# A two-block transformer stack on one core: six changes to the order of work around starts, merges, norms and the last column

## The chip, the cores and the metric

The kernel runs on one core of one Trainium2 chip. The metric is device time in microseconds (us) from launch to end. The engines are named as in the profile: PE is TensorE (PEld its weight loads), DVE is VectorE, ACT is ScalarE, POOL is GpSimd, SP is SyncE, which issues most DMAs.

## What is computed

512 tokens of width 1024 go through two blocks of two layers each, all in float32.

```python
def first_block(x, ...):          # block 1, for l in range(2)
        h = rmsnorm(x, norm1_g[l])
        p = h @ w_in[l]
        ...
        branches = jnp.stack([y_rw, y_ret, y_sg], axis=2)
        proj = jnp.einsum('bsgc,gcd->bsgd', branches, w_branch[l])
        gates = jax.nn.sigmoid(gate_logits.reshape(B, S, N_BRANCH, D_MODEL))
        x = x + jnp.sum(gates * proj, axis=2) @ w_out[l]
        x = x + conv_ffn(rmsnorm(x, norm2_g[l]), ...)
    return rmsnorm(x, final_g)
```

The three branches of block 1 are an RWKV-7 recurrence (y_rw), a chunked retention (y_ret) and a spatial gating unit (y_sg). Block 2 has five attention branches in place of these (dsa, fox, sb, nsa, mem), the same gated merge over five branches with an output projection, and no feed-forward part; it ends with a last RMSNorm, which is the result.

## The kernel before

**Products.** x lies with features on the partitions: eight tiles of 128 x 512 (features x tokens). A float32 product is made as three products of split operands: every operand is cut into an upper part (whi of a weight, shi or shl of an activation), rounded on ACT, and a lower one (wlo, slo), a subtraction on DVE. mm3 (L166) does whi x shi, whi x slo and wlo x shi into one PSUM bank, so lines L168, L169 and L170 are most of PE's work. fm_tile (L361) makes one output tile of 128 features from 8 blocks of weights, 24 matmuls over 512 tokens; fm_steps (L370) is the same as a generator. Weights come in chunks of 128 x 1024 (8 blocks) through weights (L152): a DMA on SP's queue into wraw, the cast to whi on ACT (L159), the subtraction for wlo on DVE (L160). Each of wraw, whi and wlo has two buffers.

**PSUM.** Three pools share the eight banks. In block 1 dense tiles (pm and pbr, from PM) have two banks, small products (psx, psn, psb and others, from P) four, and retention (PF) two; in block 2 PM has three and P five.

**The order of work.** In block 1 the three branches and the gates are generators that a small planner (Plan) interleaves: each step names a cost and a wait, chains that are due come first, and dense tiles fill in. PE's order there is the order in which the program issues. Everywhere else the framework orders each engine's instructions by program order and by its own model of when each would be ready; every queue then runs in that order. The casts of weights and the evacuations of dense tiles have raised priority.

**Places that the change touches.**

- The start (run, L1782): for each of the eight x tiles norm_step makes the two parts (L184, L185) and at once the square (L299, ACT) and its sum (L302, DVE); two weight chunks are loaded ahead. Then come constants, some of them through F buffers, of which there are eight and which the x tiles use too, and end_norm: the sums over features as products with ones (psn, L310), a root (ACT), a reciprocal (DVE), and a broadcast by products with the identity (psb, L317) into rb. Dense tiles are scaled with rb when they leave PSUM, so a tile's matmuls need only the parts, and its bank is free only when rb is there.
- tm_group (L379): values with tokens on the partitions, 256 features wide. Both weight chunks are loaded, and then each of four token groups gets 24 matmuls over 256 columns (12 from each chunk), a bank, and an evacuation on ACT (L788, L839). There are four such groups in each layer of block 1.
- rw_unit (L609): one of 32 units of the recurrence, each for 128 tokens of one pair of heads. Its last products are psx: for each 64-token half c (rows of the array) and head e (columns of the array) three products of 64 x 64 x 64, each of them two passes in the trace. Halves go to different banks, heads to different partitions of a bank.
- merge (L923): for each of 8 output columns c and each branch n a gate is loaded (L933), made a tanh on ACT (L936) and multiplied on DVE (L939) with pbr, a product of 12 matmuls; the branch sums are added (L943). In block 1 the third branch is the recurrence, whose last part (shl, L181) is the last thing that the planner's chains make (L739 to L757 in rw_final, with sums that are broadcast through DRAM).
- Between the blocks: ffn (L963) ends with end_norms (L325), two norms at once: psn for both sums, five small operations, psb twice, rb and rb1. Block 2 then starts with the projections misc and iq (col, L1297).
- The end: the last merge keeps its eight output columns (xlast), end_norm follows, and at L1816 each column is scaled on DVE and sent out in one DMA, on SP's and ACT's queue in turn.

## Time and profile before

| what | us |
|---|---|
| median of 3 runs | 3305.34 (3305.04 to 3309.78) |
| the profiled execution, its own time | 3305.33 |
| its span, first to last instruction | 3303.6 |
| PE busy | 3231.0 |
| DVE busy | 2188.8 |
| ACT busy | 1365.9 |
| POOL busy | 125.6 |

The span is that of one execution under the profiler; the time of the same execution is 1.7 us longer than its span. Busy times are unions of instructions on an engine. Matmuls are pipelined, so a busy PE is not PE at its peak: how far apart matmuls start tells more than how long one lasts.

### The profile page before, as it was taken

Reading aid. Unit: us, or ns where it says so; the run is one execution under the profiler, and the core shown is the slowest. Engines: PE = TensorE matmul, PEld = TensorE weight load, DVE = VectorE, ACT = ScalarE, POOL = GpSimd, SP = SyncE. Lnnn points to the kernel's source line nnn. Section 1 sums busy time; section 2 is a strip of 40 time slices with the busy share of each in tenths; the row PEclk is TensorE's granted clock in tenths of the full one; section 3 lists DMA queues with packets and bytes.
Section 4 is the critical chain, followed back from the end, with each engine's and each line's share of the span. In section 5 each row is a group of like instructions: output and inputs, shape, how many; then the busy total and the mean of one; then the engine's idle time right before and its main releaser. Section 6 shows DMA issues by size and latency. Waiting matters only on the chain.

```text
span 3303.6 us, 47422 instructions
## 1 busy us (share of the span) xinstructions
PE 3231.0 (98%) x17956; PEld 2594.5 (79%) x17960; DVE 2188.8 (66%) x4062; ACT 1365.9 (41%) x2440; POOL 125.6 (4%) x176
## 2 busy tenths in 40 slices
PE   8999999999999999999999999999999999999998
PEld 6787877888887787878888878877787888777777
DVE  6765656777537855646677446986666669866665
ACT  5433434444335333434444334344334443443443
POOL 0000000000000000000000000010003100100031
PEclk9999999999999999999999999999999999999999
DMA  4433245333433423246333437453455564533464
GB/s 146 124 94 96 74 136 170 128 107 96 137 112 105 130 75 91 80 139 189 102 99 99 150 108 212 134 159 104 121 185 197 172 170 138 152 113 121 152 209 140
DMA packets 198644, 434.75 MB, mean 132 GB/s; under 512 B 29704, under 2 KB 56456, under 8 KB 198416
## 3 DMA queue, kind: packets, MB, share of 16 engines
q1 hardware_dynamic: 197328, 429.62, 42.1%
q8 instruction: 142, 2.33, 0.3%
q0 software_dynamic: 512, 1.05, 0.1%
q10 hardware_dynamic: 576, 1.05, 0.1%
q14 instruction: 86, 0.70, 0.1%
HBM read 339.05 MB, written 61.36 MB: 121 GB/s over the span
## 4 chain that ended last, share of the span: by engine, by line
PE 84%; DVE 6%; DMA 6%; ACT 2%; issue 2%; SPq 1%; POOL 0%; DVEq 0%; ACTq 0%; POOLq 0%
PE pm L168 22%; PE pm L170 21%; PE pm L169 21%; PE psy L1152 2%; PE pbr L168 2%; PE pbr L169 2%; PE pbr L170 2%; PE pspt L1142 2%; DVE wlo L160 1%; PE psl L1124 1%; DMA sqr<-sumd 1%; PE psl L1125 1%; DMA rdw<-sumd 1%; ACT whi L159 1%; PE pssc L804 1%
## 5 line engine op out<-in xcount | busy, mean ns | idle before, releaser
L168 PE MATMUL pm<-shi,whi 128*128 128x512 f32 x3072 | 1231.7, 401 | 8.8 <-ACT whi L159 7.9
L170 PE MATMUL pm<-shi,wlo 128*128 128x512 f32 x3072 | 1207.4, 393 | 1.1 <-DVE wlo L160 1.0
L169 PE MATMUL pm<-slo,whi 128*128 128x512 f32 x3072 | 1206.1, 393 | 1.8 <-DVE slo L185 1.8
L159 ACT ACTIVATE whi<-wraw 128x1024 fp32r<-128x1024 f32 x480 | 509.3, 1061 | 884.4 <-PE pm L169 533.3
L160 DVE TENSOR_TENSOR wlo<-wraw,whi 128x1024 fp32r<-128x1024 f32 x480 | 588.1, 1225 | 206.1 <-ACT whi L159 199.6
L168 PEld LDWEIGHTS pm<-shi,whi 128*128 128x128 f32 x3072 | 578.6, 188 | 147.4 <-issue 26.8
L170 PEld LDWEIGHTS pm<-shi,wlo 128*128 128x128 f32 x3072 | 578.1, 188 | 127.6 <-DVE wlo L160 4.8
L169 PEld LDWEIGHTS pm<-slo,whi 128*128 128x128 f32 x3072 | 578.7, 188 | 117.2 <-DVE slo L185 4.4
L424 DVE TENSOR_TENSOR ev<-pm,rb 128x512 f32<-128x512 f32 x140 | 96.1, 686 | 113.6 <-PE pm L170 113.1
L894 DVE TENSOR_TENSOR gate<-pm,rb 128x512 f32<-128x512 f32 x80 | 55.1, 688 | 128.5 <-PE pm L170 128.4
L168 PE MATMUL pbr<-shi,whi 128*128 128x512 f32 x288 | 115.0, 399 | 14.0 <-ACT shl L181 10.4
L168 PE MATMUL pm<-whi,shi 128*128 128x256 f32 x384 | 115.0, 300 | 7.1 <-ACT whi L159 7.1
L169 PE MATMUL pm<-wlo,shi 128*128 128x256 f32 x384 | 111.7, 291 | 3.7 <-DVE wlo L160 3.6
L170 PE MATMUL pbr<-shi,wlo 128*128 128x512 f32 x288 | 113.1, 393 | 0.0
L169 PE MATMUL pbr<-slo,whi 128*128 128x512 f32 x288 | 113.1, 393 | 0.0
L170 PE MATMUL pm<-whi,slo 128*128 128x256 f32 x384 | 111.1, 289 | 0.0
L939 DVE SCALAR_TENSOR_TENSOR gate<-gate,pbr 128x512 f32<-128x512 f32 x128 | 85.8, 683 | 31.8 <-PE pbr L170 31.1
L943 POOL TENSOR_TENSOR gate<-gate 128x512 f32<-128x512 f32 x48 | 78.3, 1630 | 593.1 <-DVE gate L939 337.0
L936 ACT ACTIVATE gate<-gate 128x512 f32<-128x512 f32 x128 | 75.9, 626 | 42.2 <-DMA gate<-gtd 39.9
L1109 ACT ACTIVATE p<-psl,st 128x256 f32<-128x256 f32 (+3 forms) x128 | 65.2, 513 | 61.0 <-DVE st L1107 51.6
L168 PEld LDWEIGHTS pm<-whi,shi 128*128 128x128 f32 x384 | 76.0, 198 | 9.8 <-ACT whi L159 7.7
L169 PEld LDWEIGHTS pm<-wlo,shi 128*128 128x128 f32 x384 | 76.3, 199 | 4.7 <-DVE wlo L160 4.5
(506 smaller groups left out, 4465.8 us busy)
## 6 DMA issues: line engine op xcount, KB each, us to landing
wraw<-in_w_gt SPq DMA_DIRECT2D x148, 512.0 KB, 3.7
wraw<-in_w_in SPq DMA_DIRECT2D x116, 512.0 KB, 3.7
wraw<-in_f_up SPq DMA_DIRECT2D x88, 512.0 KB, 3.5
gtd<-gate SPq DMA_DIRECT2D x116, 256.0 KB, 2.0
gate<-gtd SPq DMA_DIRECT2D x116, 256.0 KB, 4.0
wraw<-in_w_br SPq DMA_DIRECT2D x44, 512.0 KB, 3.7
wraw<-in_f_dn SPq DMA_DIRECT2D x44, 512.0 KB, 3.5
wraw<-in_w_out SPq DMA_DIRECT2D x32, 512.0 KB, 3.7
```

The source lines that it names most:

```text
L159: nc.scalar.activation(hi[:, :n], raw[:, :n], AF.Copy)
L160: nc.vector.tensor_tensor(lo[:, :n], raw[:, :n], hi[:, :n].bitcast(F32), op=OP.subtract)
L168: nc.tensor.matmul(ps, lhsT=lhs[0], rhs=rhs[0], start=first, stop=False, skip_group_check=skip)
L169: nc.tensor.matmul(ps, lhsT=lhs[0], rhs=rhs[1], start=False, stop=False, skip_group_check=skip)
L170: nc.tensor.matmul(ps, lhsT=lhs[1], rhs=rhs[0], start=False, stop=last, skip_group_check=skip)
L424: self.last = self.nc.vector.tensor_tensor(t, ps, self.rb, op=OP.mult)
L936: nc.scalar.activation(g, g, AF.Tanh, scale=0.5)
L939: nc.vector.scalar_tensor_tensor(g, g, 1.0, pb, op0=OP.add, op1=OP.mult)
L943: (nc.gpsimd if self.pre and n in self.cfg.get("pa", (1, 2, 3)) else nc.vector).tensor_tensor(g, g, acc, op=OP.add)
L1109: nc.scalar.activation(p[:, :w], l, AF.Exp, bias=st[:, 0:1], accum_out=st[:, 1:2])
L1142: nc.tensor.transpose(pt_[:, b * 128:(b + 1) * 128], ps[e][:, b * 128:(b + 1) * 128], self.ident)
L1152: nc.tensor.matmul(psy[64 * e:64 * e + 64, :], lhsT=vs[e][b], rhs=pts[e][:, b * 128:(b + 1) * 128], start=first and b == 0, stop=last and ...
```

## The change

Six edits. (1) At the start the parts of all x tiles come first and the squares after them; the first two dense tiles take retention's two banks. (2) tm_group holds two banks and uses the first weight chunk for all four token groups before it takes the second. (3) psx takes two banks at once and goes through the products with head and half as the inner loops, so that products that follow each other lie in different quadrants of the array. (4) In merges of three branches the third branch's product of a column comes after the first two products of the next column; the weights are laid out in the same order. (5) end_norms moves from the end of ffn into block 2, behind the first two projection tiles. (6) The last output column and the last norm are made by halves of the tokens (finish), each half with its own sums, root, scaling and DMAs.

```diff
     def fm_steps(self, ws):
 
-        ps = self.PM(name="pm")
+        ps = self.banks.pop(0) if self.banks else self.PM(name="pm")
...
     def tm_group(self, src, evac):
...
-        ws = [self.weights(src[i], 1024) for i in range(2)]
-        for g in range(4):
-            ps = self.PM([128, 512])
-            for k in range(KD):
-                w = ws[k // 4]
-                o = (k % 4) * 256
-                hh = (self.h[k][0][:, g * 128:(g + 1) * 128], self.h[k][1][:, g * 128:(g + 1) * 128])
-                self.mm3(ps[:, :256], hh, (w[0][:, o:o + 256], w[1][:, o:o + 256]), k == 0, k == KD - 1)
-                if k == KD // 2 - 1:
+        ps = [self.PM([128, 2, 256]) for _ in range(2)]
+        for i in range(2):
+            w = self.weights(src[i], 1024)
+            for g in range(4):
+                for k in range(4):
+                    hh = [t[:, g * 128:(g + 1) * 128] for t in self.h[4 * i + k]]
+                    ww = [t[:, k * 256:(k + 1) * 256] for t in w]
+                    self.mm3(ps[g // 2][:, g % 2], hh, ww, i == 0 and k == 0 and g % 2 == 0, i == 1 and k == 3, skip=True)
+                if i and g % 2:
+                    evac(g - 1, ps[g // 2][:, 0])
+                    evac(g, ps[g // 2][:, 1])
+                if (i, g) != (1, 3):
                     yield MORE
-            evac(g, ps[:, :256])
-            yield MORE if g < 3 else TILE
+        yield TILE
...
+        psx = [self.P([128, 2, 64], "psx") for _ in range(2)]
+        for m in range(3):
+            for e in range(2):
+                for c in range(2):
+                    cs = slice(64 * c, 64 * c + 64)
+                    os = ws = slice(64 - 64 * e, 128 - 64 * e)
+                    us = slice(64 * e, 64 * e + 64)
+                    b_ = tk[cs, 0, us]
+                    o, x, y, first, last = ((0, uw[cs, e, ws], b_, True, True), (1, b_, uw[cs, e, us], True, False),
+                                            (1, tk[cs, 1, us], vp[cs, 3 * e, :], False, True))[m]
+                    nc.tensor.matmul(psx[c][os, o, :], lhsT=x, rhs=y, start=first, stop=last, skip_group_check=True)
         for c in range(2):
-            psx = self.P([128, 2, 64], "psx")
...
-                nc.tensor.matmul(psx[os, 0, :], lhsT=uw[cs, e, ws], rhs=b_, start=True, stop=True,
-                                 skip_group_check=True)
-                nc.tensor.matmul(psx[os, 1, :], lhsT=b_, rhs=uw[cs, e, us], start=True, stop=False,
-                                 skip_group_check=True)
-                nc.tensor.matmul(psx[os, 1, :], lhsT=tk[cs, 1, us], rhs=vp[cs, 3 * e, :], start=False, stop=True,
-                                 skip_group_check=True)
...
+            nc.vector.tensor_tensor(xt[:, 2 * g + c, :], psx[c][:, 0], self.ident64, op=OP.add)
+            nc.scalar.activation(cc[:, 2 * g + c, :], psx[c][:, 1], AF.Copy)
...
-        s, late = [], []
...
-        for c in range(KD):
-            acc = None
-            for n in range(nb):
-                if (c, n) in self.gd:
-                    g = self.F(name="gate")
-                    nc.sync.dma_start(g, self.gd[c, n])
-                else:
-                    g = self.gate(self.gs, "F")
-                nc.scalar.activation(g, g, AF.Tanh, scale=0.5)
-                pb = self.fm_tile(ws, ys[n], name="pbr")
-                with self.tc.high_priority(offset=self.cfg.get("hp", self.AHEAD)):
-                    nc.vector.scalar_tensor_tensor(g, g, 1.0, pb, op0=OP.add, op1=OP.mult)
-                if late and n == self.cfg.get("ln", 1):
-                    s.append(self.split(late.pop(), *stag(c - 1), scale=0.5))
-                if acc is not None:
...
-            self.dump("%ss%d_%d" % (self.pre, l, c), acc)
-            late.append(acc)
-        s.append(self.split(late.pop(), *stag(c), scale=0.5))
+        for c, n in merge_order(nb):
+            if (c, n) in self.gd:
+                g = self.F(name="gate")
+                nc.sync.dma_start(g, self.gd[c, n])
+            else:
+                g = self.gate(self.gs, "F")
+            nc.scalar.activation(g, g, AF.Tanh, scale=0.5)
+            pb = self.fm_tile(ws, ys[n], name="pbr")
+            with self.tc.high_priority(offset=self.cfg.get("hp", self.AHEAD)):
+                nc.vector.scalar_tensor_tensor(g, g, 1.0, pb, op0=OP.add, op1=OP.mult)
+            if late and n == self.cfg.get("ln", 1):
+                s.append(self.split(late.pop(), *stag(len(s)), scale=0.5))
+            if c in acc:
+                (nc.gpsimd if self.pre and n in self.cfg.get("pa", (1, 2, 3)) else nc.vector).tensor_tensor(
+                    g, g, acc[c], op=OP.add)
+            acc[c] = g
+            if n == nb - 1:
+                self.dump("%ss%d_%d" % (self.pre, l, c), g)
+                late.append(acc.pop(c))
+        for t in late:
+            s.append(self.split(t, *stag(len(s)), scale=0.5))
...
-        for c in range(KD):
+        for c in range(KD if split else KD - 1):
...
+        if not split:
+            self.finish(wo, s)
+
+    def finish(self, wo, s):
+
+        nc = self.nc
+        ww = [next(wo) for _ in range(KD)]
+        self.xlast.append(self.x_get(KD - 1))
+        x = self.xlast[-1]
+        for hf in range(2):
+            cs = slice(256 * hf, 256 * hf + 256)
+            ps = self.PM()
+            for k in range(KD):
+                self.mm3(ps[:, 0:256], ww[k], [t[:, cs] for t in s[k]], k == 0, k == KD - 1)
+            nc.vector.tensor_tensor(x[:, cs], ps[:, 0:256], x[:, cs], op=OP.add)
+            sq = self.T_(name="sql")
+            nc.scalar.activation(sq[:, 0:256], x[:, cs], AF.Square)
+            ps = self.P([128, 512], "psn")
+            for g in range(2):
+                for i, t in enumerate((self.sq[:, cs], sq)):
+                    nc.tensor.matmul(ps[:, g:g + 1], lhsT=t[:, g * 128:(g + 1) * 128], rhs=self.ones[:, 0:1],
+                                     start=i == 0, stop=i == 1, skip_group_check=True)
+            col = self.hp.tile([128, 8], F32, name="rcol", tag="rcol", bufs=2)
+            nc.scalar.activation(col[:, 4:6], ps[:, 0:2], AF.Sqrt, bias=self.eps[:, 0:1], scale=1.0 / D)
+            nc.vector.reciprocal(col[:, 0:2], col[:, 4:6])
+            ps = self.P([128, 512], "psb")
+            for g in range(2):
+                nc.tensor.matmul(ps[:, g * 128:(g + 1) * 128], lhsT=col[:, g:g + 1].to_broadcast([128, 128]),
+                                 rhs=self.ident, start=True, stop=True)
+            for c, t in enumerate(self.xlast):
+                nc.vector.scalar_tensor_tensor(t[:, cs], t[:, cs], self.vlast(c), ps[:, 0:256], op0=OP.mult, op1=OP.mult)
+                (nc.sync if c % 2 else nc.scalar).dma_start(self.out[c][:, cs], t[:, cs])
...
-        if gain1:
-            self.end_norms()
-        else:
+        if not gain1:
             self.end_norm()
...
+        self.early = []
+        if l == 0 and self.sq2 is not None:
+            self.early = [self.fm_tile(self.ws) for _ in range(2)]
+            self.end_norms()
...
-        self.end_norm(copy=gain is not None)
+        if gain is not None:
+            self.end_norm()
...
     def col(self, name, scale=None, tag="F"):
-        return self.evac2(self.fm_tile(self.ws), name, scale, tag)
+        ps = self.early.pop(0) if self.early else self.fm_tile(self.ws)
+        return self.evac2(ps, name, scale, tag)
...
                 with block(self, "act"):
                     self.begin_norm()
                     self.first = self.stream(I["w_in1"][0, 0:14])
+                    xs = []
                     for c in range(KD):
-                        self.norm_step(c, self.x_get(c), vg(0)(c), eng=nc.gpsimd if c in self.cfg.get("pe", ()) else None)
+                        xs.append(self.x_get(c))
+                        self.h.append(self.split(xs[c], tag="h", scale=vg(0)(c)))
                         if c in self.cfg.get("pr", (0, 2)):
                             self.first.prime()
+                    for x in xs:
+                        self.sq = self.add_square(self.sq, x)
+                    self.banks = [self.PF(), self.PF()]
                     self.consts()
                     self.end_norm()
                     self.am = [self.ap.tile([128, 2, 4, 128], F32, name="am%d" % i) for i in range(2)]
...
+                self.vlast = vg(40)
                 for l in range(L2):
                     self.block2_layer(l, vg(32) if l < L2 - 1 else None)
-                for c, x in enumerate(self.xlast):
-                    nc.vector.scalar_tensor_tensor(x, x, vg(40)(c), self.rb, op0=OP.mult, op1=OP.mult)
-                    (nc.sync if c % 2 else nc.scalar).dma_start(self.out[c], x)
...
-def merge_stream(w):
+def merge_order(nb):
+
+    if nb != 3:
+        return [(c, n) for c in range(8) for n in range(nb)]
+    o = []
+    for c in range(9):
+        o += [(c, 0), (c, 1)] * (c < 8) + [(c - 1, 2)] * (c > 0)
...
```

## Rows read from the trace of the kernel before

**Rows 1.** The page, sections 1 and 4: busy time; the last chain
```profile
...
PE 3231.0 (98%) x17956; PEld 2594.5 (79%) x17960; DVE 2188.8 (66%) x4062; ACT 1365.9 (41%) x2440; POOL 125.6 (4%) x176
...
PE 84%; DVE 6%; DMA 6%; ACT 2%; issue 2%; SPq 1%; POOL 0%; DVEq 0%; ACTq 0%; POOLq 0%
...
```

**Rows 2.** What PE waited for: in total, times, longest us
```profile
...
PE pm L168 <- ACT whi L159: 15.0, 4, 7.9
PE pbr L168 <- ACT shl L181: 10.4, 2, 5.4
...
PE pm L169 <- DVE wlo L160: 3.6, 2, 2.1
...
PE psx L697 <- ACT cc L704: 0.2, 1, 0.2
...
```

**Rows 3.** Busy time by stretch; third from the end: granted clock
```profile
...
123.77:129.33 5.56, 5.56 (x26) 5.56 (x27) 1.37 (x4) 1.04 (x3) 0.00 (x0) 0.50 0.54 151
1087.76:1091.89 4.13, 4.13 (x19) 4.13 (x20) 1.15 (x2) 1.40 (x4) 0.00 (x0) 0.50 0.17 46
514.66:518.45 3.79, 3.79 (x9) 3.05 (x10) 0.65 (x1) 0.38 (x1) 0.00 (x0) 0.50 0.00 0
1480.38:1484.42 4.04, 4.04 (x10) 3.18 (x11) 0.90 (x2) 0.63 (x1) 0.00 (x0) 0.50 0.00 0
1942.24:1956.53 14.29, 7.30 (x33) 7.01 (x33) 10.51 (x27) 9.26 (x18) 4.15 (x17) 0.64 0.44 139
...
```

**Rows 4.** Timeline, token-major groups: start, duration, operation, [idle before]
```profile
...
116.47 0.28 PE L168 MATMUL pm<-whi,shi 128*128 128x256 f32 x1
...
121.32 0.38 PE L168 MATMUL pm<-whi,shi 128*128 128x256 f32 x1 [3.26 <-ACT whi L159]
...
122.50 1.22 DVE L160 TENSOR_TENSOR wlo<-wraw,whi 128x1024 fp32r<-128x1024 f32 x1
...
2043.35 0.50 PE L168 MATMUL pm<-whi,shi 128*128 128x256 f32 x2 [1.19 <-ACT whi L159]
...
```

**Rows 5.** Busy time and counts of pbr, first merge to PE's stop
```profile
...
498.80:509.62 10.82, 10.80 (x45) 8.42 (x45) 1.38 (x2) 1.00 0.38 114
...
```

**Rows 6.** Timeline of DVE in the first merge
```profile
...
511.19 0.69 DVE L752 TENSOR_TENSOR y<-y,rdw 128x512 f32<-128x512 f32 x1 [3.76 <-DMA rdw<-sumd]
...
```

**Rows 7.** Timeline of PE, one unit's psx products and what follows
```profile
...
239.10 0.33 PE L697 MATMUL psx<-tk,uw 64*64 64x64 f32 x2
...
239.27 0.27 PE L697 MATMUL psx<-tk,uw 64*64 64x64 f32 x1
239.33 0.22 PE L699 MATMUL psx<-uw,tk 64*64 64x64 f32 x1
...
240.10 0.38 PE L168 MATMUL pm<-whi,shi 128*128 128x256 f32 x1
...
```

**Rows 8.** Busy time and counts of psam in one unit
```profile
...
246.08:246.50 0.42, 0.42 (x16) 0.42 (x16) 0.00 (x0) 1.00 1.02 419
...
```

**Rows 9.** Timeline of PE between the blocks
```profile
...
1945.91 3.54 PE L331 MATMUL psn<-ones,sq 128*128 128x1 f32 x16 [3.67 <-DVE sq L302]
1951.87 3.75 PE L192 MATMUL psb<-c_ident,rcol 128*128 128x128 f32 x16 [2.42 <-DVE rcol L340]
1956.53 0.47 PE L168 MATMUL pm<-shi,whi 128*128 128x512 f32 x1 [0.90 <-DVE rb L346]
...
```

**Rows 10.** Timeline, all engines, first tile of the kernel
```profile
...
13.59 0.91 SPq L155 DMA_DIRECT2D wraw<-in_w_in  x2
...
17.40 0.50 PE L169 MATMUL pm<-slo,whi 128*128 128x512 f32 x1 [0.30 <-DVE slo L185]
...
18.66 0.50 PE L169 MATMUL pm<-slo,whi 128*128 128x512 f32 x1 [0.30 <-DVE slo L185]
...
```

**Rows 11.** Timeline of DVE after the last matmul of the last column
```profile
...
3287.85 0.69 DVE L954 TENSOR_TENSOR x<-pm,x 128x512 f32<-128x512 f32 x1 [3.30 <-PE pm L170]
...
3294.66 5.36 DVE L1816 SCALAR_TENSOR_TENSOR x<-x,vecg,psb 128x512 f32<-128x512 f32 x8 [2.23 <-PE psb L317]
```

More of the change, by code (lines that the diff above doesn't have):

```diff
@@ L117, in __init__ @@
         self.dbg_outs = dbg or {}
+        self.banks = []
+        self.sq2 = None
         self.cfg = cfg or {}
@@ L925, in merge @@
         nb = len(ys)
[L926 removed]
+        s, late, acc = [], [], {}
         ws = self.stream(wbr[l])
[L928 to L947 removed]
+        for c, n in merge_order(nb):
[19 more added lines that the diff above has]
+            s.append(self.split(t, *stag(len(s)), scale=0.5))
         self.begin_norm()
@@ L1920, with merge_stream @@
 ORDER1 = [1, 2, 0]
-def merge_stream(w):
+def merge_order(nb):
[4 more added lines that the diff above has]
+        o += [(c, 0), (c, 1)] * (c < 8) + [(c - 1, 2)] * (c > 0)
+    return o
+def merge_stream(w, order=None):
     t = []
-    for c in range(8):
-        for n in range(w.shape[0]):
-            t += list(w[n][:, c * 128:(c + 1) * 128].reshape(-1, 128, 128))
+    for c, n in order or [(c, n) for c in range(8) for n in range(w.shape[0])]:
+        t += list(w[n][:, c * 128:(c + 1) * 128].reshape(-1, 128, 128))
     return np.stack(t).reshape(-1, 8, 128, 128).transpose(0, 2, 1, 3).reshape(-1, 128, 1024)
@@ L2038, in layout @@
                            for l in range(L)])
-    o["w_br1"] = np.stack([merge_stream(I["w_branch"][l][ORDER1]) for l in range(L)])
+    o["w_br1"] = np.stack([merge_stream(I["w_branch"][l][ORDER1], merge_order(3)) for l in range(L)])
     o["w_out1"] = np.stack([np.stack(_fm(I["w_out"][l], range(0, 1024, 128))) for l in range(L)])
```

9 lines of the change are left out of this document (removed).

## The prediction

> **What bounds the kernel now.** I read the page first. TensorE (PE) is busy for 98% of the span and holds 84% of the chain that ended last; no other engine holds more than 6% of it [rows 1]. So the time is PE's work plus the short stretches in which PE stands still, and an edit is worth what it takes out of those two. PE is busy for 3231.0 of 3303.6 us, so some 72 us of standing still are to be had at most, beside work that is done faster.
>
> The second view, PE's list of waits [rows 2], names the places. 15.0 us are spent waiting for the upper weight part whi, in four waits; the longest, 7.9, is the start of the kernel. 10.4 us in two waits go to shl, the parts of a recurrent branch, at the two merges of block 1. 3.6 us go to wlo.
>
> The third view, busy time and granted clock by stretch [rows 3], shows that a wait costs more than its length. [...] Work at half speed costs half of the stretch again.
>
> **What the sum is made against:** the profiled execution's 3305.33 us, its span of 3303.6 plus 1.7 outside. The median of the runs is 3305.34, the same number.
>
> **Token-major groups in chunks (tm_group).** The old order finishes one token group with both weight chunks before the next, so the second chunk is wanted after 12 matmuls: the group starts at 116.47, and PE stands at 121.32 for 3.26 us on whi and then for wlo, whose subtraction starts at 122.50 and takes 1.22 [rows 4]. The new order uses the first chunk for four token groups, 48 matmuls at a pitch of 0.12, before it wants the second. In the two layers the old order costs: whi 15.0 less the start (7.9) less one wait in block 2 (1.2, the last row of [rows 4]), so 5.9; wlo 3.6; half of the 5.56 and 4.13 us at half clock, 4.8. Together 14.3. The new need for wlo is at 116.47 + 48 x 0.12 + 0.12 = 122.35, and wlo is there at 123.72, so about 1.4 us stay in the first layer; I take 0.4 for the second. Gain 12.5, between 8 (the clock still falls) and 14.3. The number of matmuls is unchanged. Both pm banks are now held for the whole group; the first is handed back 24 matmuls, 2.9 us, before the end, which is the cover that each bank has today.
>
> **The lagging third branch (merge order).** PE does 45 pbr matmuls between 498.80 and 509.62 and then stops [rows 5]. In program order the stop would come after 12 + 12 + 9, so one tile of the next column is already done ahead of its turn. The new order places four tiles and nine matmuls before the block that is missing: 57. So only 12 matmuls more cover the wait, 12 x 0.227 = 2.7 us, not 24. The value itself cannot come earlier: the DVE chain to it starts with a multiply that waits for broadcast sums until 511.19 [rows 6]. Of two waits of 5.1 and 5.4 us some 2.3 to 2.6 stay, the stretches at half clock shrink a little (0.5 us a layer taken), and the gain is 2 x 3.2 = 6.4. Bounds: 2, if on DVE's queue the multiplies that empty the two pbr banks stand behind that waiting multiply, so that PE runs out of banks instead; 14.3, if the next tile is again done ahead and nothing is left (10.4 + half of 3.79 + 4.04).
>
> **psx by quadrants.** One unit has 12 small products of two passes each, 64 rows by 64 columns. The old order gives a quadrant of the array six passes in a row; the unit starts at 239.10 and the next product at 240.10, 1.0 us [rows 7], and all 32 units look alike. psam shows what four quadrants at once can do: 16 passes of twice the columns, four rounds, in 0.42 us, 0.105 a round [rows 8]. With the quadrants in turn psx's 24 passes make six rounds of half that, 0.32, with some 0.09 more for the first round's loads and 0.15 to the next product: 0.56. Saved 0.44 a unit, 14 in all; at most 0.5 a unit, 16. Two psx banks are now wanted at once; today PE waits for a psx bank once in 32 units, 0.2 us [rows 2]. DVE and ACT empty both halves after the last round, which is about when they empty them now.
>
> The second quadrant's first pass, L697 at 239.27, starts ahead of a pass of the first quadrant that the program puts before it, L699 at 239.33 [rows 7]: a pass that waits for its quadrant does not hold up the next one. [...]
>
> **Block 2's first tiles ahead of the norms.** PE stops at 1942.24, runs 16 passes for psn and 16 for psb with waits of 3.67 and 2.42 before them, and starts the first projection at 1956.53, held by the copy of rb and not by weights [rows 9]. The granted clock is 0.64 there [rows 3]. Of these 14.3 us the norm's own passes stay, at full clock half of 3.54 + 3.75, 3.6; the chain of small operations is covered by two tiles of 24 matmuls, 10.9 us, and behind them the third pm bank can carry the memory projection, which needs no rb. Gain 10.6 at best; I take 10, since a bank of the last FFN column must be emptied first. Bound below: 7, if psn's passes still stand on PE's queue ahead of the squares that they need. The two tiles' weight loads now stand ahead of the memory's loads on SP's queue; both were there long before PE wanted them.
>
> **The start.** In the first tile the steps are 1.26 us apart (L169 at 17.40 and 18.66), held by slo: DVE does a sum of squares between two lower parts [rows 10]. Three matmuls need 0.68, a lower part alone about 0.75. Five such steps save 2.6; with the squares off ACT's path, 3. The price is on SP's queue: the x tiles now keep all eight F buffers until their squares are done, three constants that need an F buffer stand on that queue ahead of the third and fourth weight chunk, which leave at 13.59 today [rows 10], and some 4 us later then. The first tile would end near 16, the second near 22, with the norm's passes behind it, so the third tile's chunk has some 5 us to land and be split: about covered. Two extra banks (pf) give PE two more tiles before rb. Gain 3, between 0 and 3.5.
>
> **The tail.** After the last matmul DVE adds at 3287.85; the first scaled column starts at 3294.66, eight take 5.36 [rows 11], and the span ends 3.6 later. By halves, the second half's add, square and psb shrink to about 0.6 of their length and one DVE sum goes: its chain takes about 4.8 instead of 6.8, its eight half columns about 3.0. That is 4.4 us less, against 48 matmuls at 0.12 for 24 at 0.227 (0.3 more) and 0.9 for the first half's psn: 3.2 at best. If on DVE the second half's add stands behind the first half's eight columns, it is 0.8 worse than now. I take 2.
>
> **Sum:** 12.5 + 6.4 + 14 + 10 + 3 + 2 = 47.9, so 3305.3 - 47.9 = 3257. With all the upper bounds 14.3 + 14.3 + 16 + 10.6 + 3.5 + 3.2 = 62, 3243; with all the lower ones 8 + 2 + 4.9 (rival 1) + 7 + 0 - 0.8 = 21, 3284.
>
> **Rivals.**
> 1. psx does not overlap: each product's second pass holds up the next quadrant, 12 x 0.055 + 0.04 for the first + 0.15 = 0.85 instead of 1.0 us, 4.9 us in all. Then 3266. The row at 239.27 speaks against it. Chance 0.10.
> 2. The waits move instead of going: the lagging order runs out of pbr banks (gain 2) and the clock still falls after the token-major groups (gain 8). Then 3266. For it: DVE stood idle until 511.19 [rows 6] while a pbr tile was ready to be emptied. Chance 0.17.
> 3. [...] Chance 0.13.
> 4. Slower: the two pm banks. A token-major group holds both, and if ACT empties them late the next dense tile waits. It decides from (47.9 + 6.6) / 8 = 6.8 us for each of the eight groups on. PE's longest waits are for whi and shl [rows 2] and none is for such a bank, which speaks against it. Then 3312 or more. Chance 0.04.
> 5. No change, because what is saved in block 1 is waited for later: over 41 us would have to come back, of the 72 that PE stands still in all today [rows 1]. Chance 0.03.
>
> **How the numbers follow.** The forecast, six terms of about their size (3250 to 3265), has 0.53 and is the likeliest: 3257. The range 3243 to 3280 takes in rivals 1 to 3 and most of the way to all the lower bounds. A change of 0.2%, 6.6 us, is about what a measurement can tell here. Faster holds the forecast and rivals 1 to 3, 0.93; within 0.2% 0.03; slower 0.04.
>
> **What would show it.** psx: a unit's 24 passes within some 0.4 us, four starts close together. Groups: no wait on whi over 1.5 us before a 256-column matmul, no stretch at 0.50 behind it. Merge: 57 pbr matmuls before the wait for shl, which is 2 to 3 us long. Norms: pm matmuls from 1942 on without a stop, psn among them. Start: steps under 0.9 us in the first tile. Tail: under 14 us from the last pm matmul to the end. The prediction is wrong if a wait for a pm or pbr bank appears, if the third weight chunk stops PE near 22 us, or if in block 2, whose PE order a model lays out anew, waits of several us turn up.

## The result, and the profile after

The changed kernel takes 3268.86 us (median of 4 runs, 3264.70 to 3270.00), beside 3305.19 for the kernel before: ratio 0.9887, 95% interval 0.9870 to 0.9904, so 36 us faster where 48 were forecast. That is inside the range of 3243 to 3280 and above the 3250 to 3265 that the forecast itself was given. Run again later it took 3270.88 against 3303.75, ratio 0.9903 (0.9887 to 0.9919), 33 us. The profiled execution of the first set is the fastest of its four (3264.70, span 3263.0); what it shows is 40.6 us better than the profiled execution of before, so its sums are a few us too good, and the second profiled execution (span 3271.1) stands beside it below.

The page, its busy times and its chain that ended last, as in [rows 1]:

```profile
PE 3208.0 (98%) x17992; PEld 2574.7 (79%) x17992; DVE 2187.2 (67%) x4071; ACT 1362.0 (42%) x2442; POOL 124.9 (4%) x176
...
PE 82%; DVE 8%; DMA 6%; issue 2%; ACT 2%; SPq 0%; POOL 0%; DVEq 0%; ACTq 0%; POOLq 0%
```

PE still bounds the kernel. Its busy time fell by 23.0 us (mostly psx and the stretches at half clock), its standing still by 17.6. To see where, I cut both traces at the first starts of named tiles; each length is the distance of two such starts, for both layers of block 1 together where there are two. psA is a small product of the recurrence that reads kkr; psret belongs to the retention and reads pret; psam, psu and psx belong to the 32 units; pspt is the first product of block 2's attention.

| stretch | before | after | again | gained | forecast |
|---|---|---|---|---|---|
| start to first psA | 75.76 | 74.68 | 75.40 | 1.1, 0.4 | 3 |
| psA to psret (the first token-major groups) | 149.40 | 139.36 | 141.76 | 10.0, 7.6 | 12.5 |
| psret to pbr (the 32 units) | 698.46 | 686.29 | 687.73 | 12.2, 10.7 | 14 |
| pbr to psn (merges of block 1) | 240.60 | 235.52 | 235.28 | 5.1, 5.3 | 6.4 |
| psn to the next layer's psA | 420.48 | 421.08 | 420.47 | -0.6, 0.0 | 0 |
| last psn of block 1's merges to first pspt (between the blocks) | 438.54 | 433.61 | 433.83 | 4.9, 4.7 | 10 |
| pspt to the last merge | 1129.36 | 1126.35 | 1128.12 | 3.0, 1.2 | 0 |
| last merge to the end | 150.96 | 146.11 | 148.52 | 4.9, 2.4 | 2 |

The gains add up to 40.6 and, but for rounding, 32.5, the whole difference of the spans. PE's list of waits, against [rows 2]:

```profile
PE pf L170 <- ACT whi L161: 7.0, 1, 7.0
PE pbr L170 <- DVE gate L940: 6.6, 4, 2.9
PE psA L546 <- DVE kkr L533: 5.6, 5, 1.8
PE psam L651 <- ACT rhs L635: 3.6, 4, 1.2
PE psb L194 <- DVE rcol L342: 2.6, 1, 2.6
PE psret L812 <- DVE pret L810: 2.3, 3, 1.0
...
PE pm L170 <- DVE ev L428: 1.3, 2, 0.7
...
PE pm L170 <- ACT whi L161: 0.9, 1, 0.9
```

The waits for shl are gone, and for whi there is the start and one of 0.9. Others have grown, which the kernel before had with:

```profile
PE pbr L168 <- DVE gate L939: 3.3, 3, 1.5
PE psA L542 <- DVE kkr L529: 2.9, 3, 1.5
PE psb L192 <- DVE rcol L340: 2.4, 1, 2.4
PE psam L647 <- ACT rhs L631: 1.6, 4, 0.6
PE psret L809 <- DVE pret L807: 1.1, 2, 0.7
```

For a pbr bank (gate) the kernel before waited in block 2 alone; in the changed kernel 5.8 of the 6.6 us are new, in the merges of block 1. The waits for kkr, rhs and pret have about doubled. The one for rcol is as long as before, and the waits for an emptied pm bank (ev) are new. Each marks a term that came out other than forecast.

**Merge.** Busy time and counts of pbr from the first merge to the stop, as [rows 5]; then DVE there, against [rows 6]:

```profile
486.74:498.22 11.48, 11.48 (x48) 8.98 (x48) 1.38 (x2) 1.00 0.47 122
```
```profile
499.69 0.69 DVE L755 TENSOR_TENSOR y<-y,rdw 128x512 f32<-128x512 f32 x1 [4.33 <-DMA rdw<-sumd]
500.30 0.68 DVE L940 SCALAR_TENSOR_TENSOR gate<-gate,pbr 128x512 f32<-128x512 f32 x1
```

PE stops after 48 matmuls, four tiles, and not after 57. DVE stands idle for 4.33 us in front of L755, which waits for broadcast sums, while the third and fourth tile lie finished in the two banks; the multiply that empties the third, L940, is next in DVE's queue and runs at 500.30. PE goes on at 501.13, after 2.91 us.

**Clock.** Two stretches behind the waits of the two merges, and the one between the blocks, as [rows 3] (third from the end: granted clock):

```profile
501.13:504.69 3.56, 3.56 (x9) 2.80 (x10) 3.46 (x6) 2.58 (x4) 0.00 (x0) 0.52 0.00 0
1453.60:1457.01 3.41, 3.41 (x8) 2.67 (x9) 3.31 (x6) 2.51 (x4) 0.00 (x0) 0.50 0.00 0
...
1914.45:1936.95 22.50, 19.05 (x110) 17.00 (x109) 16.27 (x34) 12.92 (x22) 4.15 (x17) 0.95 0.51 159
```

In the second of these stretches pbr matmuls of 512 columns start 0.43 us apart (1454.06, 1454.48, 1454.91), and 0.23 apart once the granted clock is 1.00 (1457.04, 1457.27). Below, a stretch at 0.50 is taken to cost half of its length, an estimate from these starts.

The stretches behind the groups' waits for whi and wlo are gone. But a group now wants its second bank 24 matmuls after its first, and waits until DVE has emptied the dense tile before it: 0.69 and 0.60 us in this trace, 0.58 and 2.48 in the second one, where a stretch at 0.50 follows the longer wait. One line of the first trace, then two of the second:

```profile
119.09 0.39 PE L170 MATMUL pm<-whi,shi 128*128 128x256 f32 x1 [0.69 <-DVE ev L428]
```
```profile
1073.47 0.39 PE L170 MATMUL pm<-whi,shi 128*128 128x256 f32 x1 [2.48 <-DVE ev L428]
...
1073.95:1077.36 3.41, 3.41 (x19) 3.41 (x18) 3.41 (x5) 3.33 (x9) 0.00 (x0) 0.50 0.50 151
```

**Groups and psA.** DVE behind the first groups, in the changed kernel and then in the kernel before:

```profile
128.77 0.75 DVE L527 SCALAR_TENSOR_TENSOR kkr<-mix,vec,sqk 128x512 f32<-128x512 f32 x1 [3.30 <-DMA sqk<-sumd]
...
133.29 0.69 DVE L533 SCALAR_TENSOR_TENSOR kkr<-kkr,sc 128x512 f32<-128x512 f32 x1
```
```profile
129.19 0.75 DVE L523 SCALAR_TENSOR_TENSOR kkr<-mix,vec,sqk 128x512 f32<-128x512 f32 x1 [4.19 <-DMA sqk<-sumd]
...
133.72 0.69 DVE L529 SCALAR_TENSOR_TENSOR kkr<-kkr,sc 128x512 f32<-128x512 f32 x1
```

PE comes to the next psA at 133.06, 8.2 us sooner than in the trace of before (141.24), but kkr, whose chain starts when broadcast sums land, is made only 0.4 us sooner. PE waits 1.07 us for it and then 1.02 for pret at 143.43: by psret 6.1 us of the 8.2 are left.

**psx.** One unit and the next product, against [rows 7]:

```profile
232.24 0.34 PE L704 MATMUL psx<-tk,uw 64*64 64x64 f32 x8
232.41 0.30 PE L704 MATMUL psx<-uw,tk 64*64 64x64 f32 x8
232.53 0.30 PE L704 MATMUL psx<-vp,tk 64*64 64x64 f32 x8
232.75 0.38 PE L170 MATMUL pm<-whi,shi 128*128 128x256 f32 x1
```

Eight passes each, four starting close together: 0.51 us from the unit's start to the next product instead of 1.00. From first to last start it is 0.36 us in 28 units, 0.47 in two, 0.86 in two, against 0.85 in all 32 before.

What takes some of it back is psam's wait. psam does not read rhs: it waits for the bank of pst, a small product of the same pool, which ACT empties into rhs and DVE into tk. The longest of the four waits, in DVE's, ACT's and PE's order:

```profile
309.81 0.69 DVE L755 TENSOR_TENSOR y<-y,rdw 128x512 f32<-128x512 f32 x1 [3.59 <-DMA rdw<-sumd]
...
315.27 0.75 DVE L630 COPY tk<-pst 128x256 f32<-128x256 f32 x2
...
316.00 0.23 ACT L635 ACTIVATE rhs<-pst 128x64 f32<-128x64 f32 x1
...
316.29 0.44 PE L651 MATMUL psam<-kr,kkr 64*64 64x128 f32 x4 [1.20 <-ACT rhs L635]
```

DVE had stood idle for 3.59 us in front of L755, for broadcast sums, and came late to all that stands behind it. The longest wait of the second layer (1.19) has the same rows in front of it, with 3.17 idle.

**Between the blocks**, PE, ACT and DVE, against [rows 9]:

```profile
1926.30 1.84 PE L333 MATMUL psn<-ones,sq 128*128 128x1 f32 x16
...
1931.04 1.06 ACT L161 ACTIVATE whi<-wraw 128x1024 fp32r<-128x1024 f32 x1 [1.44 <-PE pm L171]
1932.01 0.28 ACT L340 ACTIVATE rcol<-rcol,eps 128x4 f32<-128x4 f32 x1
1932.13 1.23 DVE L162 TENSOR_TENSOR wlo<-wraw,whi 128x1024 fp32r<-128x1024 f32 x1 [1.85 <-ACT whi L161]
...
1933.70 2.73 PE L194 MATMUL psb<-c_ident,rcol 128*128 128x128 f32 x16 [2.58 <-DVE rcol L342]
```

psn runs behind both early tiles, so the small operations only start at 1928; a weight's two parts (1.06 and 1.23 us) get in front of the last of them.

**Start.** DVE in the first tile, against [rows 10]:

```profile
12.65 0.75 DVE L187 SCALAR_TENSOR_TENSOR slo<-x,vecg,shi 128x512 fp32r<-128x512 f32 x1
13.32 0.68 DVE L304 TENSOR_TENSOR sq<-sq 128x512 f32<-128x512 f32 x1
13.92 0.74 DVE L187 SCALAR_TENSOR_TENSOR slo<-x,vecg,shi 128x512 fp32r<-128x512 f32 x1
```

A sum of squares still stands between two lower parts, 1.27 us apart, and PE's steps are as long as before.

**Tail.** DVE and PE in the last column, against [rows 11]:

```profile
3251.84 0.42 DVE L979 TENSOR_TENSOR x<-pm,x 128x256 f32<-128x256 f32 x1 [1.08 <-PE pm L172]
...
3252.29 3.22 DVE L995 SCALAR_TENSOR_TENSOR x<-x,vecg,psb 128x256 f32<-128x256 f32 x8
...
3255.64 1.07 PE L992 MATMUL psb<-c_ident,rcol 128*128 128x128 f32 x4 [1.98 <-DVE rcol L989]
3256.75 3.22 DVE L995 SCALAR_TENSOR_TENSOR x<-x,vecg,psb 128x256 f32<-128x256 f32 x8 [1.16 <-PE psb L992]
```

The second half's add stands ahead of the first half's eight columns. From the add of column 6 to the end of the span it is 17.8 us (3245.20 to 3263.0), before 21.2 (3282.41 to 3303.6); from the start of the last pm matmul it is 11.5, before 16.2.

### The profile page after: what moved, and what is told of

Read it like the earlier page. It is cut to its first block, busy times and chain, and to the rows that moved or that the text cites. A ratio compares the mean times of both kernels' runs of the same rounds, so it can differ in the third digit from the quotient of the medians.

```text
span 3263.0 us, 47497 instructions
## 1 busy us (share of the span) xinstructions
PE 3208.0 (98%) x17992; PEld 2574.7 (79%) x17992; DVE 2187.2 (67%) x4071; ACT 1362.0 (42%) x2442; POOL 124.9 (4%) x176
## 4 chain that ended last, share of the span: by engine, by line
PE 82%; DVE 8%; DMA 6%; issue 2%; ACT 2%; SPq 0%; POOL 0%; DVEq 0%; ACTq 0%; POOLq 0%
PE pm L170 21%; PE pm L172 21%; PE pm L171 21%; PE psy L1186 2%; PE pbr L170 2%; PE pbr L171 2%; PE pbr L172 2%; PE pspt L1176 2%; DVE wlo L162 2%; DMA rdw<-sumd 1%; DMA sqr<-sumd 1%; PE psl L1158 1%; PE psl L1159 1%; DMA sqk<-sumd 1%; DMA sumd<-sums 1%
## 5 line engine op out<-in xcount | busy, mean ns | idle before, releaser
L940 DVE SCALAR_TENSOR_TENSOR gate<-gate,pbr 128x512 f32<-128x512 f32 x128 | 85.7, 683 | 29.1 <-PE pbr L172 28.5
```

The source lines that it names most:

```text
L940: nc.vector.scalar_tensor_tensor(g, g, 1.0, pb, op0=OP.add, op1=OP.mult)
```

## The experiments

Two questions: is what a part gives the same by itself (four kernels made from the one before), and what holds back each term that fell short (the others, made from the changed one). All ratios are to the kernel before on the same chip. By the medians the four parts alone give 6.8, 9.0, 6.4 and 4.6 us, 26.7 together; with the tail's 3.4 and the start's 0.4 to 1.1 that makes about 31, beside the 33 and 36 of the whole. The intervals of the parts are some 3 us to either side, so no more than that can be said of how they act on each other. The start and the tail were not run alone.

**tm_only**: the chunked groups alone.

```diff
-        for g in range(4):
-            ps = self.PM([128, 512])
...
+        ps = [self.PM([128, 2, 256]) for _ in range(2)]
+        for i in range(2):
+            w = self.weights(src[i], 1024)
+            for g in range(4):
```

> The kernel before with the chunked token-major groups alone. My theory: the waits for whi and wlo and the 0.50 stretches behind them go as in the changed kernel, but they also hid the operand chains that run beside the groups, so psA (waiting for kkr) and psret (waiting for pret) stop PE about 1 us each right behind the group; net gain 5.0 us a layer, 10 in all, 3295. Rival: those two waits come from the other parts of the change; then there is no wait over 0.6 us behind the groups and the gain is 12.5 to 14, 3291 to 3293.

3296.03 us against 3302.85, ratio 0.9985 (0.9976 to 0.9994), 6.8 us where 10 were expected. The profiled execution (3303.19) lies above the median, so I read lengths, not its sum: psA to psret is 143.36, 6.0 under before. Two lines of its waits:

```profile
PE psA L544 <- DVE kkr L531: 6.9, 5, 2.3
...
PE psret L811 <- DVE pret L809: 3.4, 3, 1.4
```

The waits for kkr and pret come with this part alone (2.9 and 1.1 before, with psx alone 3.0 and 1.5): 1.44 for pret in the first layer and 2.18 for kkr in the second stand right behind the groups. Inside the groups stand waits of 0.72 and 0.84 us for the second bank. The theory holds for the waits; the term is 6 to 7 us in this kernel, less than the 10 that I read from the first trace.

**psx_only**: psx by quadrants alone.

```diff
+        psx = [self.P([128, 2, 64], "psx") for _ in range(2)]
+        for m in range(3):
+            for e in range(2):
+                for c in range(2):
...
         for c in range(2):
-            psx = self.P([128, 2, 64], "psx")
...
```

> The kernel before with psx by quadrants alone. My theory: nearly every unit saves 0.49 us from its first to its last start (0.36 instead of 0.85), 14 to 15 us in all, and psam, whose rhs comes from ACT, gives back some 2; gain 12, 3293. Rival: psx's gain is full when it is alone and what is missing in the changed kernel is eaten by the token-major groups; then 14 to 15, 3290 to 3291, and PE's wait for rhs is no longer than before.

3293.87 us, ratio 0.9971 (0.9961 to 0.9981), 9.0 us. The units save 14.7 us from first to last start (27.3 to 12.6), the stretch psret to pbr 12.4 (698.46 to 686.10). psam's waits behind ACT's rhs are 2.9 us, where the kernel before has 1.6 and the kernels with one other part 0.8 (tm_only), 0.9 (merge_only) and 0.4 (early_only). In that stretch PE stands still for 7.4 us in all instead of 6.9, and 3.41 us at 0.50 follow one of psam's waits (1.19), which cost 1.7 by the estimate above; together that is 2.2 of the 2.3 us that are missing. So some 2 us go back with this part alone, as the theory has it, but what psam waits for is a bank and not an operand. Whether that is because psx now holds two banks at once or because PE comes sooner was not separated.

**merge_only**: the lagging order alone.

```diff
+    for c in range(9):
+        o += [(c, 0), (c, 1)] * (c < 8) + [(c - 1, 2)] * (c > 0)
```

> The kernel before with the lagging branch order alone. My theory: PE stops after 48 pbr matmuls for a bank and not after 57 for shl, because DVE's multiply that empties the third tile stands behind the multiply that waits for broadcast sums; the wait is 2.9 us in each layer, one stretch of 3.4 us at 0.50 follows instead of 6.8, and the gain is 2.4 + 2.8 = 5 us, 3300. Rival: the bank wait comes from the earlier arrival of PE in the changed kernel; alone, PE gets to 57 matmuls and waits 2 to 3 us for shl.

3296.50 us, ratio 0.9978 (0.9970 to 0.9987). The two merges take 235.38 instead of 240.60. PE waits 2.95 and 2.81 us for a bank, in these two merges never for shl; 3.41 us at 0.50 follow each time. The theory holds, and the bank wait belongs to this part.

**early_only**: two tiles of block 2 ahead of the norms, alone.

```diff
+            self.early = [self.fm_tile(self.ws) for _ in range(2)]
+            self.end_norms()
```

> The kernel before with two tiles of block 2 ahead of the norms alone. My theory: psb still waits 2.6 us for rcol, because a weight split (1.06 on ACT, 1.23 on DVE) stands in its chain, and the granted clock falls for 3.4 us behind it; the stretch between the blocks gains 5 us, and some 3 us more come in the next 100 us of block 2 where the weights are now ahead; 8 in all, 3297. Rival: the 3 us in block 2 belong to another part; then 5, 3300.

3298.30 us, ratio 0.9986 (0.9977 to 0.9995). The stretch between the blocks is 433.45, as in the changed kernel; psb waits 2.58. From pspt to the last merge it takes 1127.40, 2.0 less than before, but the three kernels without this part lie at 1125.58 to 1128.74. So those 3 us are the spread of executions and the rival's 5 are right.

**banks4**: more banks for the branch tiles, from the pair that stands free (PF).

```diff
-            pb = self.fm_tile(ws, ys[n], name="pbr")
+            pb = self.fm_tile(ws, ys[n], name="pbr", ps=self.PF(name="pbr") if not self.pre and i % 2 else None)
```

> The changed kernel with four banks for the branch tiles of block 1's merges: every second one from the pair called pf, which stands free there. My theory: the wait for a bank (2.9 us after 48 matmuls) is only the first of two; without it PE does 57 pbr matmuls and stops 3 to 5 us for shl, since nothing makes the value come earlier, and the time stays within 2 us a layer of the changed kernel's, 3265 to 3270. Rival: the bank was the only thing missing, shl is ready when PE gets there, and both the 2.9 us and the 0.50 stretch behind it go, 4.6 us a layer, 9 in all: 3260.

3269.97 us, ratio 0.9907 (0.9890 to 0.9923). PE now does 58 pbr matmuls, the 57 that were forecast and one of the next tile, and then:

```profile
503.69 0.53 PE L170 MATMUL pbr<-shl,whi 128*128 128x512 f32 x1 [4.08 <-ACT shl L183]
```

4.30 in the second layer. The merges take 238.16, 2.6 more than with the bank wait. The theory holds: behind the bank stood shl. L755 starts 13.78 and 14.00 us after the first pbr matmul, where it was 12.39 and 12.69 in the kernel before; from there to the end of shl on ACT it is 4.0 instead of 3.4, because one emptying multiply stands between the steps.

**lag2_banks4**: and the third branch two columns behind.

```diff
-    for c in range(9):
-        o += [(c, 0), (c, 1)] * (c < 8) + [(c - 1, 2)] * (c > 0)
+    for c in range(8 + 2):
+        o += [(c, 0), (c, 1)] * (c < 8) + [(c - 2, 2)] * (c >= 2)
```

> The kernel with four branch banks, and in addition the missing branch two columns behind instead of one: 81 pbr matmuls ahead of shl. My theory: 81 x 0.227 = 18.4 us cover the 15.8 us from the first pbr matmul to shl that the kernel before shows; neither a bank nor shl stops PE for over 0.5 us in the two merges of block 1, no 0.50 stretch follows, and the stretch from the first pbr to psn is 4.6 us a layer shorter than in the changed kernel: 113.2 instead of 117.8; 3260 in all. Rival: with three sums open the gates' loads run out of F buffers, and PE stops for a gate or a bank instead; the stretch is no shorter than 116.

3262.20 us, ratio 0.9880 (0.9865 to 0.9894). The merges take 115.27 and 114.64: 2.5 and 3.1 less, not 4.6. No wait for shl or a bank over 0.5 us there and no stretch at 0.50, but a new one:

```profile
507.71 0.50 PE L172 MATMUL pbr<-shl,wlo 128*128 128x512 f32 x1 [1.43 <-DVE wlo L162]
```

That lower weight part is computed behind the same idle DVE (L755 starts at 501.99 after 4.97 us) and the chain that follows. The mechanism was right; the size missed the third thing in that queue.

**psn_mid**: psn between the two early tiles.

```diff
+        self.early.append(self.fm_tile(self.ws))
         col, r1 = (self.hp.tile([128, 8], F32, name="rcol", tag="rcol", bufs=2) for _ in range(2))
...
-            self.early = [self.fm_tile(self.ws) for _ in range(2)]
+            self.early = [self.fm_tile(self.ws)]
             self.end_norms()
```

> The changed kernel with psn between the two early tiles instead of behind both. My theory: the 2.6 us wait of psb for rcol is a chain of small operations that starts only when psn is done, behind both tiles; psn one tile earlier puts 5.4 us more in front of psb, the wait goes and with it the 3.4 us at 0.50: 4.3 us less in the stretch from block 1's last merge to block 2's first pspt (429.3 instead of 433.6). Rival: psn's operands (the squares of the last column) are not there one tile earlier, or psb now stands ahead of the memory projection with nothing behind it that is ready: then one wait takes the other's place, and the stretch is 432 to 435.

3264.83 us, ratio 0.9891 (0.9877 to 0.9906). The stretch is 429.21, where 429.3 was expected:

```profile
1927.20 1.84 PE L333 MATMUL psn<-ones,sq 128*128 128x1 f32 x16
...
1934.49 1.95 PE L194 MATMUL psb<-c_ident,rcol 128*128 128x128 f32 x16
```

psb waits for nothing and no stretch at 0.50 follows. So the order of two things was what the term lacked. The ratio is within the intervals of the changed kernel's; it is the length that shows the gain.

**kkr_first**: three operations for psA ahead on DVE.

```diff
+        bd = kkr
+        with self.tc.high_priority(offset=self.AHEAD):
+            nc.vector.tensor_tensor(kr[:, :, 0, :], g4(kkr), g4(e0), op=OP.mult)
+            nc.vector.scalar_tensor_tensor(bd, a, 1.0, kkr, op0=OP.add, op1=OP.mult)
+            nc.vector.scalar_tensor_tensor(bd, bd, 0.5, ei, op0=OP.mult, op1=OP.mult)
         kd = k
...
```

> The changed kernel with the three DVE operations that psA waits for (kr, and the two multiplies that make the last kkr) in front of others on DVE's queue. My theory: the part of the token-major groups' gain that did not arrive went into psA's waits for kkr (5.6 us in five waits, and a 0.50 stretch behind one), because the chain to kkr starts at the landing of broadcast sums, which the change does not move; DVE does two to three operations of others between them, 1.2 to 1.9 us, so the waits shrink to under 0.5 us each and 4 to 6 us are gained: 3263 to 3265 against 3269. Rival: psA then comes earlier but the next thing (pret, rhs) is as late as before, and the time is the same within 1.5 us.

3262.75 us, ratio 0.9886 (0.9871 to 0.9901). psA's waits fall from 5.6 us to 0.7; the stretches up to the first psA of each layer are 1.3 to 1.5 us shorter (73.34 against 74.68 from the start; 57.50 against 59.02 from the second layer's norm). Behind them others grow:

```profile
PE pm L170 <- DVE ev L428: 3.6, 2, 1.9
...
PE psA L547 <- DVE kkr L532: 0.7, 3, 0.3
```

psA to psret in both layers is 139.54, between the 139.36 and 141.76 of the changed kernel: there the rival holds, and what comes next takes the time (the second pm bank, 3.6 us in the two groups, where the two traces of the changed kernel have 1.3 and 3.1). The theory holds for the waits. Of the time 2.3 us arrive by the profiled executions (3264.70 to 3262.40); the ratio is no clearer, its interval overlaps with both of the changed kernel's (0.9887 and 0.9903). So the size stays open, and 4 to 6 us are not shown.

**all_three**: lag2_banks4, psn_mid and kkr_first together; **after_again**: the changed kernel beside it.

> The changed kernel with the two-column lag on four banks, psn between the early tiles, and the operations for kkr in front, together. My theory: the three sit in different stretches and add up as each measured by itself: first pbr to psn 2.5 to 3.1 us shorter in each layer, the stretch between the blocks 4.3, the two stretches up to the first psA 1.3 to 1.5 each: 12 to 13 us below the changed kernel on the same chip. Rival: they share DVE's queue, on which more work is now put in front, and the waits for wlo that two of them brought (1.3 to 1.4 us each) grow; then under 9 us.

> The changed kernel once more, beside the others on one chip and beside more runs of the kernel before. My theory: 36 us under before (39 us of stage gains, less 2 to 3 that its token-major groups lose in executions with a later landing of the broadcast sums); ratio 0.988 to 0.990. Rival: the profiled execution is the usual one, 40 us, ratio 0.9877 or less.

all_three: 3257.30 us, ratio 0.9859 (0.9841 to 0.9876). after_again: 3270.88, ratio 0.9903 (0.9887 to 0.9919). The intervals do not meet: 13.6 us less than the changed kernel on the same chip, as expected, and the fastest version here. By lengths: between the blocks 4.6 (433.83 to 429.28); merges 2.9 (235.28 to 232.43), less than the 5.6 by themselves: in the first layer 3.41 us at 0.50 follow the wait for wlo of 1.48, which is 1.7, and in the second a wait of 0.62 us for a weight has come in front of it; up to the first psA 2.0 and 1.2. after_again came out below the expected 36, with 33.

**psx_cme** and **psx_emc**: two quadrants take turns, then the other two. The edit of psx_cme, and then that of psx_emc:

```diff
-        for m in range(3):
-            for e in range(2):
-                for c in range(2):
+        for c in range(2):
+            for m in range(3):
+                for e in range(2):
```
```diff
-        for m in range(3):
-            for e in range(2):
+        for e in range(2):
+            for m in range(3):
                 for c in range(2):
```

> The changed kernel with psx's products in the order of halves of tokens, then product, then head: only two quadrants, which share their rows of the array and differ in columns, take turns; the second pair follows. My theory: a pass waits only for its own quadrant, a quadrant takes a pass every 0.058 us, and about three waiting passes may stand ahead of one that starts: each pair needs six rounds, 0.35, the second pair starts when the first one's last passes wait, some 0.2 to 0.3 later; 0.55 to 0.65 us from the first start of a unit to its last instead of 0.36, 6 to 9 us more in all. [...]

> The same with head first, then product, then half of tokens: the two quadrants that take turns share their columns and differ in rows. My theory: as with the other pair, 0.55 to 0.65 us from first to last start. [...]

One time each, 3271.75 and 3275.31, which says little; the units say more. One unit of psx_cme and one of psx_emc, from the first passes to the next product:

```profile
208.73 0.33 PE L704 MATMUL psx<-tk,uw 64*64 64x64 f32 x4
...
209.41 0.33 PE L625 MATMUL pst<-c_ident,kr 128*128 128x128 f32 x1
```
```profile
212.60 0.33 PE L704 MATMUL psx<-tk,uw 64*64 64x64 f32 x4
...
213.27 0.33 PE L625 MATMUL pst<-c_ident,kr 128*128 128x128 f32 x1
```

From first to last start it is 0.52 or 0.53 us in 30 units of psx_cme and in 28 of psx_emc, with sums of 17.1 and 17.7 against 12.7. Pairs that share rows and pairs that share columns are alike, a little faster than expected, and but for two units of psx_emc (0.88) nothing is near the 0.85 of the kernel before. The three waiting passes of the theory can be read from that kernel: in the unit of [rows 7] the second quadrant's first pass starts at 239.27, and three of the first quadrant's passes after it, at 239.33, 239.38 and 239.44.

## Why the forecast was right in direction and 12 us too good

**psx (14).** Right in mechanism: 14.5 us inside the units. The step that failed is that the banks of small products cost nothing: the prediction weighed two psx banks against one wait of 0.2 us for such a bank and let DVE and ACT empty them "about when they empty them now". psam's waits for a bank grew by 2.0 us in the changed kernel; psx_only shows that this part alone gives some 2 us back. Rival 1 is out.

**Groups (12.5).** The waits on whi and wlo and the slow stretches went as described, with 0.16 us left on wlo, but "14.3 together" counted the stops of PE as if nothing else were waited for in them. They also covered the DRAM trip of the sums for kkr, which lands when it did before (128.77, before 129.19), and the emptying of the bank that a group takes second; that both pm banks are held was booked at no cost. The new waits in these stretches are 4.6 us in the first trace (kkr 2.1, the second bank 1.3, pret 1.0, wlo 0.2). In the second they are 5.3 (the bank 3.1, pret 1.6, wlo 0.7), and 1.7 more for the 3.41 us at 0.50 behind the bank. With the old waits and half of the old stretches at half clock, 14.6 us by the trace, that leaves the 10.0 and 7.6 measured; the one stretch of 3.41 us at 0.50 behind a layer's first psA stands in all three traces. tm_only shows that these waits come with the part; in kkr_first, with kkr's waits gone, the bank's are 3.6 us and the stretches no shorter.

**Merge (6.4).** Measured 5.1 to 5.3. The size is near by accident: the mechanism was the one that I had put under the lower bound, two banks and DVE's queue. Its price there, a gain of 2, was wrong too: the waits fell from 5.06 and 5.36 us to 2.91 and 2.89, which is 4.6, and the work at half clock behind them from 3.79 and 4.04 to 3.41 each, which is another 0.5. banks4 shows that the 57 matmuls were counted rightly and that "2.3 to 2.6 stay" was wrong: 4.1 to 4.3 stay, because the chain to shl got later too. 1.3 to 1.4 us of that lie in the trip of the sums and 0.6 in the emptying multiply between the chain's steps, less 0.2 for the one matmul more; why the trip took longer stays open.

**Norms (10).** Measured 4.7 to 4.9. The failed step is "the chain of small operations is covered by two tiles". The chain starts at psn, and psn stood behind both tiles, so only the memory projection, 24 matmuls at 0.12, covered it. The lower bound of 7 assumed psn too early; that it might be too late was not weighed. psn_mid shows this with its 429.21.

**Start (3).** Measured 0.4 to 1.1, part of it the first matmul's own spread (6.9 to 8.4 us in the kernels with the old start). From the first matmul until PE comes to psA it is 66.7 us before and 66.1 in both traces, so 0.6 is the part's own. The step that failed is that a new program order is a new order on DVE. The steps are 1.27 us as before, since the sums of squares still run between the lower parts. Why they are put there was only argued (the framework orders each queue by its own model) and not tried; the cause stays open.

**Tail (2).** Mis-sized by the choice: the best case, 3.2, was right, with 3.4 measured from column 6 to the end (3.7 in the second trace).

Rival 2's first half happened, with a gain of 5 and not 2. Its second half did not in the first trace, and in the second trace once, behind a bank and not behind a weight. So the time lies near the 3266 of rivals 1 and 2 without either being what happened: the terms fell short by one to five us each, all but the tail, whose 1.4 us more and the 1.2 to 3.0 of block 2, which no term forecast, made up for part of it.

Rival 4's bank waits are there, 0.7 and 0.6 us (2.5 at most in the second trace), far from 6.8 us a group. Against this rival the prediction said that none of PE's waits was for such a bank; the kernel before had three, 3.3 us in all, in block 2.

Of the signs that the prediction named, those of psx and of the tail came, and that of the groups' whi. Those of merge, norms and start did not. A wait for a pm or pbr bank, by which it wanted to be called wrong, appeared in every merge of block 1 and in the first group of each layer; a stop at the third weight chunk and new waits of several us in block 2 did not.

## What to carry to other kernels

Before a wait is booked as a gain, look at what lands inside it: a chain that ends in that window, one with a DMA trip above all, can be the next wait. Here PE came to psA 8.2 us sooner and kkr's sums landed 0.4 us sooner. When two engines are coupled by a few banks, read the queue of the engine that empties them: here L755 waited for a DMA with DVE idle for 4.33 us, the multiply that empties a bank ran behind it, and PE stood still for 2.91. A producer of small sums has to stand in front of the work that is to cover it, not behind: psn one tile earlier took the stretch between the blocks from 433.61 to 429.21 us.

## What the runs showed of the hardware that was not expected

In psx's units, with four quadrants in turn, the six passes of a quadrant start 0.06 us apart after a first step of 0.11, all 24 passes within 0.36 us (the changed kernel's unit at 232.24). The two quadrants that share rows took as long as the two that share columns: 0.52 us from first to last start for either order (psx_cme, psx_emc), 0.36 for four at once (the changed kernel), 0.85 with six passes of a quadrant in a row (the kernel before).

In these traces stops of about the same length were not always followed by a lower granted clock. In the kernel before it stayed at 1.00 after a stop of 1.72 us for psu (1308.63) and after one of 1.47 for a pbr bank (2494.82), while 3.41 us at 0.50 followed one of psA's of 1.47 (1039.38); in the changed kernel the same followed one of psA's of 1.79 (1025.59), and in all_three's merge one of 1.48. So stops of 1.5 to 1.8 us cost 1.7 us more here, by the estimate of half of 3.41, or nothing.
